# Two transformer blocks with 32 experts on one core: the last pairs of experts in another order, and part of the last normalisation on GpSimd and ScalarE

## The chip, the core and the metric

The kernel runs on one NeuronCore of a Trainium2 chip. Its engines are TensorE (PE, matrix products), VectorE (DVE), ScalarE (ACT), GpSimd (Pool) and SyncE (SP, which here issues DMAs). The metric is the device time of one execution in microseconds (us), smaller is better.

## What is computed

The reference runs two blocks over 512 tokens of 1024 numbers in float32. The first is a mixer block of depth 2, the second has two kinds of attention and ends with a mixture of 32 experts, a sum and a last normalisation. Only this end matters here:

```python
def _rmsnorm(x, g):
    x32 = x.astype(jnp.float32)
    y = x32 * lax.rsqrt(jnp.mean(x32 * x32, axis=-1, keepdims=True) + EPS)
    return (y * g.astype(jnp.float32)).astype(x.dtype)
...
    for e in range(N_EXPERTS):
        he = jax.nn.silu(xt @ w_gate[e]) * (xt @ w_up[e])
        y = y + combine[:, e:e + 1] * (he @ w_down[e])
    return y
...
        x = x + y.reshape(B, T, D)
    return _rmsnorm(x, final_norm)
```

Each token goes to two of the 32 experts.

## The kernel before

The experts are worked through one after the other, in a list sorted so that each has room for 128, 96, 64 or 32 of its tokens. Weights come by DMA from SP's queue some experts ahead, the tokens of an expert by an indirect DMA from Pool's queue. The names used below:

- `gu(e)`: the gate and up products of expert `e`. For a small expert the result `pgu` is split over groups of rows and copied to `eg` by ACT (line 1843).
- `fold(e)`: PE transposes `eg` into `pfold` (line 1850), DVE sums it to `ef` (line 1852), ACT takes a tanh, and DVE makes the hidden row `eh` in two operations (lines 1861, 1862).
- `turn(e)`: PE transposes the gathered tokens of the next expert.
- `pair(e)`: the down products of two experts of the same size, `pyf` (line 1890). ACT scales them into `ys` (line 1897) and DVE makes a second tile with what the first lost in rounding, called the correction below (line 1899). Experts with 32 rows fill a quarter of such a tile each, so the pairs 28 and 29 and 30 and 31 share one.
- `add(n)`: takes up to `n` items off a list. An item is one full tile of results and one of the four tiles of 128 tokens: four PE products with a selection matrix, `psel` (line 1917), and two DVE additions to the tokens `xk` (line 1919).
- `back_add(t)`: two DVE additions of rows that the larger experts scattered to memory (line 2053).
- `finish`: for each of four tiles of tokens the last adds, then ACT's sum of squares (line 1931). Behind the fourth tile `FT` puts the inverse root, ten small DVE operations in `rsq` (lines 233 to 242), and then for each tile one DVE operation that multiplies by the root and the final weights `fin` into `fo` (line 1939), and the DMA of `fo` to the output from SP's queue.

From expert 3 on the order of PE is that of the program, written by hand; a scheduler arranges the other engines' operations and PE's after the last pair. Each engine executes its own list strictly in order. After the last tile comes a loop over experts that overflowed (`overflow`), which all engines enter and leave together.

Of the kernel before, what the change touches and what calls it, by code (L numbers as in the profile page):

```python
# [14 lines left out]
AF = mybir.ActivationFunctionType  # L15
OP = mybir.AluOpType
# [8 lines left out]
NE = 32  # L25
# [4 lines left out]
UNIT = 1040  # L30
PTC = 2
PS2 = (3, 2, 2)
FT = ((0, 4, 3),)
HB = 2

# [77 lines left out]
class K:  # L113
# [40 lines left out]
    def pb(self, name="pb"):  # L154
        return self.ps.tile([128, 512], F32, name=name, tag="A", bufs=PS2[0]) if self.single else self.pa(name)[:, :512]

# [6 lines left out]
    def pt(self, name="ptr"):  # L163
        return self.ps.tile([128, 512], F32, name=name, tag="T", bufs=PS2[1] if self.single else 2)

    def pc(self, name="pc"):
        return self.ps.tile([128, 512], F32, name=name, tag="C", bufs=PS2[2] if self.single else 1)

# [1752 lines left out]
    def finish(self, add):  # L1921

        nc = self.nc
        raw = self.eraw
        fs = raw("fs")[:, :8].rearrange("p (a t) -> p a t", a=2)
        os = []
        for t in range(4):
            add(t)
            x = self.xk[:, t, :]
            o = raw("fo")  # L1930
            nc.scalar.activation(o, x, AF.Square, accum_out=fs[:, 0, t:t + 1])
            os.append(o)
            for a, b, at in FT:
                if at != t:
                    continue
                self.rsq(fs[:, 1, a:b], fs[:, 0, a:b], 1.0 / D, EPS)
                for u in range(a, b):
                    o, rs = os[u], fs[:, 1, u:u + 1]
                    nc.vector.scalar_tensor_tensor(o, self.xk[:, u, :], rs, self.fin, op0=OP.mult, op1=OP.mult)  # L1939
                    nc.sync.dma_start(self.out[0, u * 128:(u + 1) * 128, :], o)  # L1940

    def moe(self):
        nc, I, sp, tc = self.nc, self.I, self.sp, self.tc
# [25 lines left out]
        def load(e):  # L1969
            if e + LA < NE:  # L1970
                U[e + LA] = self.ex_load(e + LA, w_of(0, e + LA), w_of(1, e + LA))
            if e + WH < NE:
                Dn[e + WH] = self.ex_wd(w_of(2, e + WH))
# [5 lines left out]
        def turn(e):  # L1979
            if e < NE:  # L1980
                X[e] = self.ex_turn(xgs[e % 2], mp, cap[e], e < 2)
# [13 lines left out]
        def gu(e):  # L1995
            if cap[e] > 64:
                Hs[e] = self.ex_gu(U[e], X[e], mp)
            else:
                G[e] = self.ex_half(U[e], X[e], mp, cap[e])

        def fold(e):
            if cap[e] <= 64:
                Hs[e] = self.ex_fold(G[e], mp, cap[e])
# [22 lines left out]
        def pair(e):  # L2026

            n = cap[e]
            q, b, sel, parts = S.pop(n, (0 if n > 32 else nm, 0, None, None))
            if b == 0:  # L2030
                sel = mp.tile([128, 512], F32R, name="sel", tag="sel", bufs=SB)
                self.ex_select(sel, by[:, 0, q:q + 1])
                parts = [mp.tile([128, 1024], F32, name="ys", tag="ys", bufs=YB).bitcast(F32R) for _ in range(2)]
            r = slice(b, b + 2 * n)
            py = self.ex_few([Dn[e - 1], Dn[e]], [Hs[e - 1], Hs[e]], n)
            self.ex_parts(py, by[r, 1, q:q + 1], [p[r] for p in parts])
            if b + 2 * n < 128:
                S[n] = q, b + 2 * n, sel, parts
            else:
                S[n] = q + 1, 0, None, None  # L2040
                return sel, parts, 128
# [3 lines left out]
        def back(t):  # L2045

            for k in range(2):
                y = B[t, k] = self.eraw("yb")
                nc.sync.dma_start(y, self.yd[k * 512 + t * 128:k * 512 + t * 128 + 128, :])
# [12 lines left out]
        def add(n):  # L2062

            for x in waiting[:n]:
                self.ex_add(*x)
            del waiting[:n]

        def step(e):
            nonlocal full
            load(e)  # L2070
            if e + 1 < NE:
                gu(e + 1)
            full = None
            if cap[e] > 64:
                scatter(e)
            elif cap[:e + 1].count(cap[e]) % 2 == 0:
                full = pair(e)
            turn(e + 2)
            gather(e + 4)
            add(2 if cap[min(e + 1, NE - 1)] > 32 else 1)  # L2080
            if e + 1 < NE:
                fold(e + 1)
            if e == 1:
                rows_by()
            if e == 15:
                self.route_extra(mp)
            if RB <= e <= RB + 1:
                back(e - RB)
            if RB < e <= RB + 2:
                back_add(e - RB - 1)  # L2090
            if full and e + 1 < NE:
                waiting.extend(full + (t,) for t in range(4))
# [3 lines left out]
        with tc.manual_schedule(engines={mybir.EngineType.PE}):  # L2096
            for e in range(3, END):
                step(e)
            load(END)
            for t in (2, 3):  # L2100
                back(t)
            for e in range(END + 1, NE):
                gu(e)
                turn(e + 1)
                add(1)
                fold(e)
            add(4)
            pair(NE - 3)
            full = pair(NE - 1)

        def last(t):
# [78 lines left out]
```

## Time and profile before

| | before |
|---|---|
| median of 3 runs | 1414.97 us (1413.94 to 1420.77) |
| the profiled execution | 1415.46 us |
| its span in the trace | 1413.6 us |
| PE, DVE busy | 1291.6 us (91%), 947.3 us (67%) |
| ACT, Pool busy | 611.2 us (43%), 311.0 us (22%) |

The span runs from the first instruction of the program to the last; all times below count from its start. A timeline row gives start, length, engine, line, operation, output and inputs, shapes and number of operations, and in brackets how long the engine stood idle before it and what ended that.

### The profile page before, as it was taken

What the parts mean: (1) busy time and instruction counts of PE and PEld (TensorE: products, weight loads), DVE (VectorE), ACT (ScalarE), POOL (GpSimd) and SP (SyncE); (2) the same over time, 40 slices, a digit from 0 to 9 for tenths busy, and PEclk for the clock granted to TensorE, in tenths of its full rate; (3) what the DMA queues carried; (4) which work ended last, traced back from release to release, by engine and by line L of the source; (5) the groups of instructions that cost most, each with busy time, mean ns of one, the idle gap of its engine ahead of it and who ended that gap; (6) DMA issues with size and microseconds to landing.
All of it is one profiled execution on the core that took longest, in us unless ns stands there. A gap on an engine that the chain in (4) does not pass through costs nothing. (4 is left out here: it accounts for less than half of the span.)

```text
span 1413.6 us, 22394 instructions
## 1 busy us (share of the span) xinstructions
PE 1291.6 (91%) x7974; PEld 1026.3 (73%) x7974; DVE 947.3 (67%) x2113; ACT 611.2 (43%) x1197; POOL 311.0 (22%) x412
## 2 busy tenths in 40 slices
PE   4999999999989999799999999999999799989792
PEld 2888778877768788677877778787788766765461
DVE  5789998566743689998775554676667723554565
ACT  4554165445641564256573334776654211112122
POOL 5333032322220233133322110211110121111100
PEclk9999999999999999999999999999999799989996
DMA  9643355435132344426144355324424799998992
GB/s 343 159 134 109 97 150 156 132 109 172 60 134 64 98 128 146 136 55 160 31 134 148 112 192 152 87 73 139 137 73 168 258 383 383 371 373 325 395 407 83
DMA packets 166772, 246.18 MB, mean 174 GB/s; under 512 B 46788, under 2 KB 102810, under 8 KB 166660
## 3 DMA queue, kind: packets, MB, share of 16 engines
q1 hardware_dynamic: 161116, 234.95, 49.9%
q0 software_dynamic: 4864, 7.66, 2.0%
q10 hardware_dynamic: 680, 2.13, 0.4%
q8 instruction: 64, 1.05, 0.3%
q14 instruction: 48, 0.39, 0.1%
HBM read 220.69 MB, written 32.28 MB: 179 GB/s over the span
## 5 line engine op out<-in xcount | busy, mean ns | idle before, releaser
L185 DVE TENSOR_TENSOR wlo<-wraw,whi 128x1024 fp32r<-128x1024 f32 (+3 forms) x98 | 118.2, 1212 | 59.5 <-ACT whi L184 59.0
L184 ACT ACTIVATE whi<-wraw 128x1024 fp32r<-128x1024 f32 (+3 forms) x98 | 100.7, 1036 | 102.3 <-PE pout L223 42.7
L221 PE MATMUL pcm<-hTh,whi 128*128 128x256 f32 (+1 forms) x288 | 102.1, 355 | 8.4 <-DVE oa L531 4.3
L571 DVE SCALAR_TENSOR_TENSOR za<-zp,vec,za 128x783 f32<-128x783 f32 (+1 forms) x120 | 108.9, 915 | 0.5
L923 POOL TENSOR_SCALAR P<-P,ll 128x768 f32<-128x768 f32 (+1 forms) x80 | 73.5, 924 | 159.7 <-DVE ll L922 142.6
L223 PE MATMUL pcm<-hTh,wlo 128*128 128x256 f32 (+1 forms) x288 | 98.4, 342 | 0.1
L222 PE MATMUL pcm<-hTl,whi 128*128 128x256 f32 (+1 forms) x288 | 97.9, 340 | 0.0
L185 DVE TENSOR_TENSOR PTl<-pPT,PTh 128x512 fp32r<-128x512 f32 x104 | 70.3, 684 | 25.2 <-ACT PTh L184 24.6
L921 ACT ACTIVATE P<-pS,nm 128x768 f32<-128x768 f32 (+1 forms) x80 | 65.0, 816 | 36.2 <-DVE nm L919 30.7
L184 ACT ACTIVATE PTh<-pPT 128x512 fp32r<-128x512 f32 x104 | 60.7, 596 | 45.3 <-PE pPT L936 41.1
L1812 POOL DMA_INDIRECT xg<-h2d,tok x32 | 31.5, 983 | 219.9 <-PE pturn L1796 165.1
L1418 POOL TENSOR_SCALAR P<-P,l 128x384 f32<-128x384 f32 (+1 forms) x64 | 33.2, 534 | 185.8 <-DVE l L1417 168.7
L919 DVE TENSOR_REDUCE nm<-pS 128x1 f32<-128x768 f32 (+1 forms) x80 | 66.0, 843 | 9.3 <-PE pS L223 8.5
L221 PEld LDWEIGHTS pcm<-hTh,whi 128*128 128x128 f32 x288 | 54.7, 190 | 16.3 <-DVE oa L531 4.9
L221 PE MATMUL pcm<-hT0h,whi 128*128 128x512 f32 x144 | 59.3, 412 | 7.9 <-DVE oa L531 5.8
L936 PE MATMUL pPT<-ident,P 128*128 128x128 f32 x416 | 62.5, 279 | 0.9 <-DVE PTl L185 0.4
L223 PEld LDWEIGHTS pcm<-hTh,wlo 128*128 128x128 f32 x288 | 54.6, 190 | 6.4 <-DVE wlo L185 0.6
L968 POOL TENSOR_TENSOR oa<-oa,ot 64x256 f32<-64x256 f32 x40 | 37.4, 935 | 97.4 <-DVE ot L967 94.1
L222 PEld LDWEIGHTS pcm<-hTl,whi 128*128 128x128 f32 x288 | 54.8, 190 | 5.1 <-issue 0.5
L222 PE MATMUL pcm<-hT0l,whi 128*128 128x512 f32 x144 | 58.3, 405 | 0.0
L223 PE MATMUL pcm<-hT0h,wlo 128*128 128x512 f32 x144 | 58.2, 404 | 0.0
L1829 PE MATMUL pgu<-exT,eraw 128*128 128x128 f32 x448 | 55.8, 289 | 0.0
(552 smaller groups left out, 3645.2 us busy)
## 6 DMA issues: line engine op xcount, KB each, us to landing
wraw<-in_w_in_dram SPq DMA_DIRECT2D x56, 512.0 KB, 4.6
eraw<-in_w_expert_gate_dram SPq DMA_DIRECT2D x52, 512.0 KB, 10.1
eraw<-in_w_expert_up_dram SPq DMA_DIRECT2D x52, 512.0 KB, 10.4
wraw<-in_w_mod_dram SPq DMA_DIRECT2D x48, 512.0 KB, 5.6
wl<-in_w_expert_down_dram SPq DMA_DIRECT2D x32, 512.0 KB, 6.4
wh<-in_w_expert_down_dram SPq DMA_DIRECT2D x32, 512.0 KB, 11.0
wraw<-in_w_out_dram SPq DMA_DIRECT2D x24, 512.0 KB, 3.6
wraw<-in_w_expert_gate_dram SPq DMA_DIRECT2D x12, 512.0 KB, 13.1
```

Source lines behind the costliest of these rows:

```text
L184: nc.scalar.activation(hi, src, AF.Copy)
L185: return (eng or nc.vector).tensor_tensor(lo, src, hi.bitcast(F32), op=OP.subtract)
L221: mm(out, lhs[0], rhs[0], start=start, stop=False)
L222: mm(out, lhs[0], rhs[1], start=False, stop=False)
L223: mm(out, lhs[1], rhs[0], start=False, stop=stop)
L571: nc.vector.scalar_tensor_tensor(a[:, :nz], z[:, k:k + nz], cfw[:, i, k:k + 1], a[:, :nz], op0=OP.mult, op1=OP.add)
L919: nc.vector.tensor_reduce(nm, S, axis=AX.X, op=OP.max, negate=True)
L921: nc.scalar.activation(P, S, AF.Exp, bias=nm, accum_out=l)
L923: nc.gpsimd.tensor_scalar(P, P, l, 0.5, op0=OP.mult, op1=OP.mult)
L936: nc.tensor.transpose(p[:, jj, i * 128:(i + 1) * 128], Ps[i][:, (j + jj) * 128:(j + jj + 1) * 128], self.ident)
L968: nc.gpsimd.tensor_tensor(o, o, t, op=OP.mult)
L1829: self.last = self.nc.tensor.matmul(p[:, s, c, :], gu[2 * s + k // 4][:, k % 4, c * 128:(c + 1) * 128], x[:, k, :], start=(k == 0), stop=( ...
```

## The change

In the loop over the last three experts, each step that still has another expert behind it now takes two items off the list instead of one. The last step takes none; the pair of experts 28 and 29 is done there, before the last folding, and what is left of the list behind it. In `finish`, for the first two of the four tiles, Pool multiplies the tokens by the final weights as soon as the square is taken (in the same tile `fo`, which the square leaves), and when the root is there ACT scales that product. The other two tiles are as before.

```diff
+FV = (0, 0, 1, 1)
...
             nc.scalar.activation(o, x, AF.Square, accum_out=fs[:, 0, t:t + 1])
+            if not FV[t]:
+                nc.gpsimd.tensor_tensor(o, x, self.fin, op=OP.mult)
             os.append(o)
...
                     o, rs = os[u], fs[:, 1, u:u + 1]
-                    nc.vector.scalar_tensor_tensor(o, self.xk[:, u, :], rs, self.fin, op0=OP.mult, op1=OP.mult)
+                    if FV[u]:
+                        nc.vector.scalar_tensor_tensor(o, self.xk[:, u, :], rs, self.fin, op0=OP.mult, op1=OP.mult)
+                    else:
+                        nc.scalar.activation(o, o, AF.Copy, scale=rs)
                     nc.sync.dma_start(self.out[0, u * 128:(u + 1) * 128, :], o)
...
             for e in range(END + 1, NE):
                 gu(e)
                 turn(e + 1)
-                add(1)
+                if e < NE - 1:
+                    add(2)
+                else:
+                    pair(NE - 3)
                 fold(e)
-            add(4)
-            pair(NE - 3)
+            add(9)
             full = pair(NE - 1)
```

PE's list from the adds of expert 30's step to the end of the last pair, before:

```order
L1917 MATMUL psel<-ys,sel 128x512 x4
L1850 MATMUL pfold<-ident,eg 128x128 x4
L1840 MATMUL pgu<-eraw,exT 32x256 x16
L1917 MATMUL psel<-ys,sel 128x512 x4
L1850 MATMUL pfold<-ident,eg 128x128 x4
L1917 MATMUL psel<-ys,sel 128x512 x8
L1890 MATMUL pyf<-wh,eh 32x512 x4
L1890 MATMUL pyf<-wl,eh 32x512 x4
L1890 MATMUL pyf<-wh,eh 32x512 x4
L1890 MATMUL pyf<-wl,eh 32x512 x4
```

and now:

```order
L1918 MATMUL psel<-ys,sel 128x512 x8
L1851 MATMUL pfold<-ident,eg 128x128 x4
L1841 MATMUL pgu<-eraw,exT 32x256 x16
L1891 MATMUL pyf<-wh,eh 32x512 x4
L1891 MATMUL pyf<-wl,eh 32x512 x4
L1851 MATMUL pfold<-ident,eg 128x128 x4
L1918 MATMUL psel<-ys,sel 128x512 x4
L1891 MATMUL pyf<-wh,eh 32x512 x4
L1891 MATMUL pyf<-wl,eh 32x512 x4
```

Lines of the changed kernel are higher by one here. The first pair's down products (`pyf`) stand behind the last gate and up product and ahead of the last folding (`pfold`); four of the adds' products (`psel`) stand between the folding and the last pair, where before there were twelve around the folding. The step before, for expert 29, has eight such products instead of four in the same way.

DVE's list from the last folding's sum to the adds of the last pairs, before:

```order
L1852 TENSOR_REDUCE ef<-pfold 128x4x32
L1919 TENSOR_TENSOR xk<-psel,xk 128x512
L1861 SCALAR_TENSOR_TENSOR eh<-eh,ef 128x64
L1919 TENSOR_TENSOR xk<-psel,xk 128x512
L1862 TENSOR_TENSOR eh<-ef,eh 128x64
L1919 TENSOR_TENSOR xk<-psel,xk 128x512 x2
L1899 SCALAR_TENSOR_TENSOR ys<-pyf,by,ys 64x512 x4
L1919 TENSOR_TENSOR xk<-psel,xk 128x512 x4
L2053 TENSOR_TENSOR xk<-xk,yb 128x1024 x4
```

and now:

```order
L1853 TENSOR_REDUCE ef<-pfold 128x4x32
L1920 TENSOR_TENSOR xk<-psel,xk 128x512
L1900 SCALAR_TENSOR_TENSOR ys<-pyf,by,ys 64x512 x2
L1862 SCALAR_TENSOR_TENSOR eh<-eh,ef 128x64
L1920 TENSOR_TENSOR xk<-psel,xk 128x512
L1863 TENSOR_TENSOR eh<-ef,eh 128x64
L1900 SCALAR_TENSOR_TENSOR ys<-pyf,by,ys 64x512 x2
L1920 TENSOR_TENSOR xk<-psel,xk 128x512 x4
L2059 TENSOR_TENSOR xk<-xk,yb 128x1024 x4
```

The first pair's two corrections (`ys`) stand ahead of both operations of the last hidden row (`eh`), where before all four corrections came behind it. On Pool two products `fo<-xk,fin` of 128x1024 stand behind the last gather and nothing but the loop's end follows them; on ACT two scalings of `fo` follow the four squares.

## Rows read from the trace of the kernel before

**Rows 1.** Timeline of PE, the last pairs of experts.

```profile
1373.26 1.93 PE L1840 MATMUL pgu<-eraw,exT 128*32 128x256 f32 x32
1375.12 1.19 PE L1917 MATMUL psel<-ys,sel 128*128 128x512 f32 x4
1376.16 0.60 PE L1850 MATMUL pfold<-ident,eg 128*128 128x128 f32 x4
1376.51 2.09 PE L1917 MATMUL psel<-ys,sel 128*128 128x512 f32 x8
1378.53 1.07 PE L1890 MATMUL pyf<-wh,eh 128*32 128x512 f32 x8
...
1380.27 1.04 PE L1890 MATMUL pyf<-wh,eh 128*32 128x512 f32 x8
```

**Rows 2.** Timeline of DVE, from the last folding to the scattered rows.

```profile
1377.09 0.68 DVE L1852 TENSOR_REDUCE ef<-pfold 128x128 f32<-128x512 f32 x1
1377.69 0.68 DVE L1919 TENSOR_TENSOR xk<-psel,xk 128x512 f32<-128x512 f32 x1
1378.29 0.22 DVE L1861 SCALAR_TENSOR_TENSOR eh<-eh,ef 128x64 f32<-128x64 f32 x1
...
1379.02 0.22 DVE L1862 TENSOR_TENSOR eh<-ef,eh 128x64 f32<-128x64 f32 x1
...
1381.96 1.51 DVE L1899 SCALAR_TENSOR_TENSOR ys<-pyf,by,ys 64x512 fp32r<-64x512 f32 x2 [1.53 <-ACT ys L1897]
1383.66 1.54 DVE L1899 SCALAR_TENSOR_TENSOR ys<-pyf,by,ys 64x512 fp32r<-64x512 f32 x2 [0.19 <-ACT ys L1897]
1385.23 2.48 DVE L1919 TENSOR_TENSOR xk<-psel,xk 128x512 f32<-128x512 f32 x4
1387.63 4.62 DVE L2053 TENSOR_TENSOR xk<-xk,yb 128x1024 f32<-128x1024 f32 x4
```

**Rows 3.** Timeline of DVE: a root at the start of the kernel, and the end.

```profile
15.44 0.91 DVE L235 TENSOR_SCALAR hrs<-rt 128x2 int32<-128x2 int32 x1
...
1395.86 0.17 DVE L233 TENSOR_SCALAR rv<-fs 128x4 f32<-128x4 f32 x1 [1.22 <-ACTq L2129]
...
1397.86 4.87 DVE L1939 SCALAR_TENSOR_TENSOR fo<-xk,fs,fin 128x1024 f32<-128x1024 f32 x4
```

**Rows 4.** Stretches: PE, PEld, DVE, ACT, POOL busy (operations), PE's clock, DMA share, GB/s.

```profile
1400.00:1405.00 5.00, 0.00 (x0) 0.00 (x0) 2.73 (x3) 0.00 (x0) 0.00 (x0) 0.50 1.02 406
...
1390.70:1413.60 22.90, 0.00 (x0) 0.00 (x0) 10.47 (x20) 2.30 (x4) 0.00 (x0) 0.50 0.23 92
```

**Rows 5.** Timeline of ACT, the last pairs and the first square.

```profile
1380.55 1.38 ACT L1897 ACTIVATE ys<-pyf,by 64x512 fp32r<-64x512 f32 x2 [2.48 <-PE pyf L1890]
1382.24 1.39 ACT L1897 ACTIVATE ys<-pyf,by 64x512 fp32r<-64x512 f32 x2 [0.31 <-PE pyf L1890]
1386.55 1.06 ACT L1931 ACTIVATE fo<-xk 128x1024 f32<-128x1024 f32 x1 [2.92 <-DVE xk L1919]
```

**Rows 6.** Groups of Pool's instructions by form: count, busy us, mean ns, idle before.

```profile
L624 POOL TENSOR_TENSOR g<-g,scv 128x768 f32<-128x768 f32 x2 | 3.7, 1831 | 14.8 <-DVE g L531 14.8
...
L624 POOL TENSOR_TENSOR g<-g,scv 128x512 f32<-128x512 f32 x2 | 2.5, 1273 | 1.7 <-DVE g L531 1.7
```

**Rows 7.** Timeline of DVE and Pool from 57.0 to 61.2.

```profile
57.09 1.22 DVE L425 TENSOR_TENSOR hTl<-x,hTh 128x1024 fp32r<-128x1024 f32 x1
57.47 3.83 POOL L867 TENSOR_TENSOR ra<-lat,tabk 128x32 f32<-128x32 f32 x1 [9.99 <-ACT lat L456]
...
60.23 0.96 DVE L185 TENSOR_TENSOR wlo<-wraw,whi 128x768 fp32r<-128x768 f32 x1
```

**Rows 8.** Timeline of DVE and Pool from 535.7 to 538.

```profile
535.93 1.55 POOL L853 TENSOR_TENSOR kt<-krot,hr 128x256 f32<-128x256 f32 x1 [3.61 <-DVE hr L242]
536.92 1.11 DVE L852 TENSOR_TENSOR kt<-kt,hr 128x512 f32<-128x512 f32 x1
```

**Rows 9.** All instructions on the tile `kt`: DVE's, ns least/median/most, first and last start.

```profile
L852 DVE TENSOR_TENSOR kt<-kt,hr x12: 679/693/1109, 79.9 to 587.9; 128x512 f32<-128x512 f32 x12
```

## The prediction

> **What bounds the kernel now.** The page's totals decide nothing here, since the change touches only the end, so I went to the timeline of the last 40 us, engine by engine. TensorE (PE) goes without a pause from experts to token adds and to the down products of the last two pairs [rows 1]. Then VectorE (DVE) runs the end: from the corrections of those pairs at 1381.96 on its operations stand almost back to back, with one gap of 1.53 us before them and one of 0.19 us between the pairs [rows 2]. The inverse root starts at 1395.86 and the four normalised tiles at 1397.86 [rows 3]. After that the writes to memory are the limit: from 1400 to 1405 they move 406 GB/s at a full DMA share [rows 4]. So there are two questions: when does DVE get to 1397.86, and when can the first write be issued?
>
> **Part 1: the order of the last pairs.** No operation is added or removed; eight PE products for adds move earlier and the pair of experts 28 and 29 moves ahead of the last folding. I walk PE and then DVE with the gaps of the rows. Eight add products instead of four hold PE 2.02 us (1376.51 to 1378.53) instead of 1.04 (1375.12 to 1376.16), so each of two steps is 0.98 later and the last gate-and-up product starts at 1373.26 + 1.96 = 1375.22 [rows 1]. It takes 1.86 (to 1375.12 before), so the moved pair's down products start at 1377.08, 1.45 earlier than 1378.53. They take 1.74 (1378.53 to 1380.27), the folding starts at 1378.82 instead of 1376.16, and it is done 0.60 later, at 1379.42 [rows 1].
>
> Now DVE, which executes in the order shown above: reduction, add, both row corrections of the moved pair, first half of the last hidden row, add, second half. The reduction goes at 1379.42, the add at 1380.02 and free again at 1380.62, each 0.60 after the one before [rows 2]. The corrections need ACT's copies, which come 2.02 after the products start (1378.53 to 1380.55) and take 1.38 [rows 1, 5]: ready at 1380.48, so they cost no wait. They occupy 1.51, to 1382.13 [rows 2]. Hidden row and add take 0.73 (1378.29 to 1379.02) and the second half of the hidden row 0.22 [rows 2]: the last hidden row is ready at 1383.08 instead of 1379.24. Before, the last pair's products started at 1380.27 because PE was busy until then [rows 1]; now they start at about 1383.1, because PE waits for DVE. From there the chain is the old one (1.97 to ACT's copies, 1.42 to the corrections, 1.57 to the adds [rows 1, 2, 5]), so everything from 1385.23 on comes **2.84 us later** (1383.11 less 1380.27). What was meant to be pulled ahead is pulled ahead, but its 1.51 us on DVE now stands in front of the hidden row on which the last pair hangs. Nothing hides it: DVE stands idle afterwards, waiting for the last pair.
>
> PE stands idle for some 2.7 us in this wait. Its clock can fall in it: from 1390.7 on, when PE has no more products, the granted clock is 0.50, which is 1.2 GHz [rows 4]. If the last pair's products ran at that level instead of 2.4 GHz they would take twice their 1.74 us. So this term lies between 0 and 1.74. I take 0, because the products come at the end of the idle stretch and not long after it, and keep 1.74 for the range.
>
> **Part 2: the products on Pool.** Two tiles' multiplications by the final weights go to Pool, which is idle after its last gather, and they need no scale, so they can run while DVE adds. The trace has no Pool product of 128x1024; 128x512 takes 1.27 and 128x768 takes 1.83 [rows 6], 0.56 more for each 256 columns, so I take 2.39 each. The first may start when the first tile's square is done, at 1387.61 (1386.55 + 1.06 [rows 5]) and a little for its read-out, just as DVE begins the four adds of the scattered rows (1387.63, 4.62 us for four [rows 2]). Both engines then read two operands from SBUF. The trace shows what that does, in two ways. At 57.47 a Pool product of 32 columns took 3.83 us, until the last of four such DVE operations (57.09 to 60.23) was over; those were not held up, the first took 1.22 and the last 0.96 [rows 7]. At 535.93 Pool got in between two DVE operations: it took 1.55, and DVE's second took 1.11 [rows 8], where the median of 12 is 0.69 [rows 9]. So they exclude each other, and who gets the turn decides the price.
>
> I take the first way: Pool is shut out until DVE's four adds end at 1392.25 (1387.63 + 4.62). The next four DVE adds read one operand from PSUM, and Pool runs beside them. Its two products then end at 1392.25 + 4.78 = 1397.03. The inverse root would start at 1395.86, and its small steps wait too: at 15.44 one of them took 0.91 [rows 3] beside a Pool product, where the first step at the end takes 0.17 [rows 3]. So the root starts at 1397.03: **1.17 us later**. The bounds are 0 (Pool disturbs nothing) and 4.78 (both products go ahead of a DVE add and DVE waits their whole length).
>
> The Trainium skill, on its page "SBUF — State Buffer", section "Who interferes with whom", says that a DVE instruction with two SBUF inputs contends with a GpSimd instruction that reads SBUF, and that whichever issues first holds the shared ports for its whole instruction. By that rule Pool, which asks before each following add, would get its turn twice and the term would be 4.78. The rows at 57.47 speak against first come, first served; those at 535.93 agree with it.
>
> **Part 3: the end.** ACT scales the two products where DVE took 1.22 us each (4.87 for four [rows 3]). ACT's square over the same 128x1024 takes 1.06 [rows 5], so the first tile is ready **0.16 earlier**, and the second 1.06 after it. Two of four DVE operations, 2.44 us, fall away, but this is worth nothing: a tile of 0.52 MB takes 1.29 us to write at 406 GB/s [rows 4], so the second to fourth tiles wait for the writes, not for an engine. SP's queue holds the same four writes in the same order; no DMA is added. If Pool were late, ACT's scaling and all four writes behind it on SP would wait, but Pool ends before the root does. What follows the last write until 1413.6 is unchanged.
>
> **The sum.** 2.84 + 1.17 - 0.16 = +3.85 us. The profiled execution took 1415.46, 0.49 above the median, and would take 1419.3; against the median of 1414.97 I forecast 1418.8.
>
> **The rivals.**
> Pool gets one turn. The first product goes between two adds, as at 535.93, and DVE is 2.39 late; the second ends at 1397.03, before the root then starts at 1398.25, and costs nothing. 2.84 + 2.39 - 0.16 = +5.07: 1420.0. For it: Pool asks almost as the first add begins (1387.61 and 1387.63 [rows 2, 5]), and where it was shut out at 57.47 it had asked 0.38 us after the operation then running. Against it: at 57.47 three changes from one DVE operation to the next went by without a turn [rows 7].
>
> Pool gets two turns, and the kernel is **slower**. Place: the four adds of scattered rows; price 2 x 2.39; it decides from the point where both products stand ahead of an add. 2.84 + 4.78 - 0.16 = +7.46: 1422.4, which is 0.53% more. For and against as above, only twice.
>
> Pool disturbs nothing, because its read and DVE's happen not to meet: 2.84 - 0.16 = +2.68: 1417.7. Against it: the long operations of [rows 7, 8].
>
> The gain that the change is made for. If the hidden row is not held up (because the products or copies come earlier than I reckon, so that DVE's corrections fall into an idle time), the gaps of 1.53 and 0.19 vanish and Pool is free: -1.72 - 0.16 = -1.88: 1413.1. Against it: DVE's order is fixed, and the corrections stand ahead of the hidden row in it.
>
> That the split does not do what it says is in the forecast already: two of four DVE operations go, and the writes keep the end where it was.
>
> **How the numbers follow.** Forecast 0.40, one turn 0.25, two turns 0.13, no disturbance 0.12, gain 0.10. The clock adds up to 1.74 to each but the last. A measurement of this kernel can tell about 0.5% from no change, 7.1 us here. Slower by more needs two turns (0.10 of its 0.13) or one turn with most of the clock's loss (5.07 + 1.74, and a little noise: 0.03): 0.13. Faster by more has no case; 0.02 for what I do not see. The rest, 0.85, is no change. The range leaves out most of the gain below, and above it the two turns with a slower clock: 1414.2 to 1422.8.
>
> **What would show it.** Right: the moved pair's products near 1377.1, the last pair's near 1383.1 with PE idle for over 2 us before it, and DVE idle for about 3.5 us before the last corrections; the first Pool product far longer than 2.4 us, the adds of scattered rows still 1.14 apart, the root held back by about a microsecond; writes at 406 GB/s from end to end. Wrong in part 1 if the last pair's products start before 1381. Wrong in part 2 if an add of scattered rows takes over 2 us, or if Pool's products last 2.4 us from the start and no DVE operation is longer.

## The result, and the profile after

| | before | changed |
|---|---|---|
| median | 1416.68 us (20 runs, 1413.07 to 1422.79) | 1425.74 us (20 runs, 1419.85 to 1429.86) |
| the profiled execution | 1415.46 us | 1429.09 us |
| its span | 1413.6 us | 1427.3 us |

The ratio is 1.0055, 95% interval [1.0042, 1.0068]: the change makes the kernel some 7.8 us slower (5.9 to 9.6 by the interval). The two medians lie 9.06 us apart. I had forecast +3.85 us, with a range up to 1422.8, so the forecast and the range were both wrong. The rival "Pool gets two turns" (+7.46) is what happened.

The two profiled executions cannot be compared by their spans. The program is the same up to the step of expert 29, and yet that step's gate and up products start 6.26 us later in the profile after. The first row is before, the others are after.

```profile
1365.18 1.93 PE L1840 MATMUL pgu<-wraw,exT 128*32 128x256 f32 x32
```

```profile
1371.44 1.93 PE L1841 MATMUL pgu<-wraw,exT 128*32 128x256 f32 x32
...
1383.13 1.04 PE L1891 MATMUL pyf<-wh,eh 128*32 128x512 f32 x8
...
1384.96 0.66 PE L1851 MATMUL pfold<-ident,eg 128*128 128x128 f32 x4
...
1386.47 1.04 PE L1891 MATMUL pyf<-wh,eh 128*32 128x512 f32 x2
1389.40 0.63 PE L1891 MATMUL pyf<-wh,eh 128*32 128x512 f32 x3 [1.88 <-DVE eh L1863]
```

From here on I measure everything from the start of these products and call what follows the **tail**: 48.45 us before (1413.6 less 1365.18) and 55.84 after. The difference of 7.39 us is the effect of the change in these two executions, and it lies inside the interval of the ratio. The timeline of DVE after shows both places where it comes from:

```profile
1385.65 0.69 DVE L1853 TENSOR_REDUCE ef<-pfold 128x128 f32<-128x512 f32 x1 [2.10 <-PE pfold L1851]
1386.26 0.68 DVE L1920 TENSOR_TENSOR xk<-psel,xk 128x512 f32<-128x512 f32 x1
1386.86 1.50 DVE L1900 SCALAR_TENSOR_TENSOR ys<-pyf,by,ys 64x512 fp32r<-64x512 f32 x2
1388.28 0.21 DVE L1862 SCALAR_TENSOR_TENSOR eh<-eh,ef 128x64 f32<-128x64 f32 x1
1388.52 0.69 DVE L1920 TENSOR_TENSOR xk<-psel,xk 128x512 f32<-128x512 f32 x1
1389.13 0.21 DVE L1863 TENSOR_TENSOR eh<-ef,eh 128x64 f32<-128x64 f32 x1
1392.80 1.54 DVE L1900 SCALAR_TENSOR_TENSOR ys<-pyf,by,ys 64x512 fp32r<-64x512 f32 x2 [3.45 <-ACT ys L1898]
1394.37 2.48 DVE L1920 TENSOR_TENSOR xk<-psel,xk 128x512 f32<-128x512 f32 x4
1396.77 8.91 DVE L2059 TENSOR_TENSOR xk<-xk,yb 128x1024 f32<-128x1024 f32 x4
1405.60 2.47 DVE L1920 TENSOR_TENSOR xk<-psel,xk 128x512 f32<-128x512 f32 x4
1409.28 0.17 DVE L234 TENSOR_SCALAR rv<-fs 128x4 f32<-128x4 f32 x1 [1.22 <-ACT fo L1932]
```

First place: the moved pair's corrections (1386.86) stand ahead of the last hidden row (1389.13). Two of the last pair's sixteen products go at 1386.47 already; the others wait for that row, PE idles for 1.88 us, and they start 17.96 us into the tail (1389.40 less 1371.44). Before, the last pair's products started 15.09 into it (1380.27 [rows 1] less 1365.18). That is 2.87 us later, and DVE then idles for 3.45 us. Second place: the four adds of scattered rows take 8.91 us where before they took 4.62 [rows 2]. The timeline in narrower windows shows the four one by one, and then Pool's two products:

```profile
1396.77 1.22 DVE L2059 TENSOR_TENSOR xk<-xk,yb 128x1024 f32<-128x1024 f32 x1
1397.90 3.36 DVE L2059 TENSOR_TENSOR xk<-xk,yb 128x1024 f32<-128x1024 f32 x1
1401.18 3.35 DVE L2059 TENSOR_TENSOR xk<-xk,yb 128x1024 f32<-128x1024 f32 x1
1404.46 1.21 DVE L2059 TENSOR_TENSOR xk<-xk,yb 128x1024 f32<-128x1024 f32 x1
```

```profile
1396.92 3.26 POOL L1934 TENSOR_TENSOR fo<-xk,fin 128x1024 f32<-128x1024 f32 x1 [25.80 <-ACT fo L1932]
1400.14 3.31 POOL L1934 TENSOR_TENSOR fo<-xk,fin 128x1024 f32<-128x1024 f32 x1
```

Read them together. Pool's first product asks at 1396.92, while the first add runs. When that add ends, at 1397.99 (1396.77 + 1.22), Pool is served (I call this being let in, or getting a turn): its product ends at 1400.18, 2.2 us later, and only then does the second add proceed, which takes 3.36 instead of 1.22. Pool's second product asks at 1400.14, waits for the second add and is served ahead of the third. A row's length holds the waiting too, on both engines.

The clock (as a share of 2.4 GHz) and the writes, in windows of the profile after, with the columns of [rows 4]:

```profile
1383.13:1389.40 6.27, 4.39 (x30) 1.59 (x22) 4.03 (x9) 2.11 (x4) 0.00 (x0) 1.00 0.57 226
1389.40:1396.77 7.37, 6.03 (x28) 2.79 (x28) 3.91 (x7) 2.44 (x4) 0.00 (x0) 1.00 0.02 8
...
1413.50:1418.50 5.00, 0.00 (x0) 0.00 (x0) 0.26 (x1) 0.03 (x1) 0.00 (x0) 0.50 1.02 406
```

The granted clock stays at its upper level of 2.4 GHz through PE's wait and behind it, and the writes again run at 406 GB/s, as in [rows 4].

### The profile page after: what moved, and what is told of

Read it like the earlier page. It is cut to its first block, busy times and chain, and to the rows that moved or that the text cites. A ratio compares the mean times of both kernels' runs of the same rounds, so it can differ in the third digit from the quotient of the medians.

```text
span 1427.3 us, 22401 instructions
## 1 busy us (share of the span) xinstructions
PE 1298.4 (91%) x7974; PEld 1032.0 (72%) x7974; DVE 949.4 (67%) x2111; ACT 613.2 (43%) x1199; POOL 318.4 (22%) x414
```

## The experiments

One table for all, from the traces. "Pair" is the start of the last pair's products (in the new order without the two that are done early), "adds" the length of the four adds of scattered rows, "root" the start of the inverse root; pair, root and the end of the tail count from the start of expert 29's gate and up products. A run without a ratio was executed once, with its profile.

| run | pair | adds | root | tail | ratio to before [95%] |
|---|---|---|---|---|---|
| before | 15.09 | 4.62 | 30.69 | 48.45 | |
| changed | 17.96 | 8.91 | 37.84 | 55.84 | 1.0055 [1.0042, 1.0068] |
| order alone | 17.96 | 4.62 | 33.55 | 51.31 | 1.0026 [1.0009, 1.0042] |
| split alone | 15.09 | 8.91 | 34.97 | 52.98 | 1.0024 [1.0003, 1.0044] |
| one product | 15.09 | 6.76 | 32.83 | 50.53 | |
| asked later | 15.09 | 8.91 | 34.97 | 52.98 | 1.0029 [1.0006, 1.0051] |
| held | 15.09 | 4.62 | 30.68 | 50.15 | |
| one operand | 15.09 | 6.30 | 32.35 | 50.37 | |
| free adds | 15.09 | | 33.78 | 51.80 | |
| parts after | 16.40 | 4.62 | 32.02 | 49.78 | |
| pieces | 15.09 | 6.20 | 32.26 | 50.28 | |
| two early adds | 16.03 | | 31.44 | 49.22 | 1.0008 [0.9993, 1.0024] |
| one early add | 15.10 | | 29.78 | 47.55 | 0.9996 [0.9979, 1.0012] |
| small piece first | 15.09 | 8.90 | 34.96 | 53.06 | |

### The two halves apart

Order alone is the changed kernel with the old end:

```diff
-FV = (0, 0, 1, 1)
+FV = (1, 1, 1, 1)
```

> The new order of the last pairs, with all four tiles' products of the last norm by DVE as before. Measured from the start of the gate and up product of expert 29, the tail lasts 48.4 us in the kernel before and 55.8 us in the change. Theory (the two halves of the change add up, 2.9 us from the order and 4.3 us from Pool): last pair's down products 2.8 us later than before, the four adds of scattered rows 4.6 us together as before, tail 51.2 us (+2.8), median about +3 us. Rival (the order costs nothing, it is all Pool): tail 48.4 us. Rival (the order brings a lower clock behind it): tail above 52 us with a granted clock below 1.00 ahead of the last adds.

Split alone is the changed kernel with the loop of before:

```diff
-                if e < NE - 1:
-                    add(2)
-                else:
-                    pair(NE - 3)
+                add(1)
                 fold(e)
-            add(9)
+            add(4)
+            pair(NE - 3)
```

> The order of before, with only the products of tiles 0 and 1 on Pool and their scaling on ACT. Theory (Pool takes two turns between the four adds): adds 8.9 us together instead of 4.6, the root 4.3 us later, tail 52.7 us (+4.3), median about +4.5 us. The step that I forecast (Pool is shut out until the adds end): adds 4.6 us, root +1.2 us, tail 49.6 us. Rival (Pool takes its turns only because the new order brings the adds to a moment that suits it): adds 4.6 to 6.8 us here.

The rows of the order alone, PE's and DVE's:

```profile
1384.06 0.63 PE L1891 MATMUL pyf<-wh,eh 128*32 128x512 f32 x3 [1.88 <-DVE eh L1863]
```

```profile
1391.42 4.62 DVE L2059 TENSOR_TENSOR xk<-xk,yb 128x1024 f32<-128x1024 f32 x4
```

Measured: +2.86 us from the order and +4.53 us from the split (51.31 and 52.98 less 48.45). Their sum is 7.39, what the whole change costs: the two halves do not help or hinder each other. Of the split's 4.53, 4.28 are in the root's start already (34.97 less 30.69), all of it in the four adds; the last 0.25 come behind the root. I did not follow them up; with one product on Pool (below) they are not there (17.70 us from the root to the end, 17.76 before). The rows of DVE and Pool in the split alone are those of the changed kernel again, though its adds begin at another moment of the program:

```profile
1385.84 8.91 DVE L2059 TENSOR_TENSOR xk<-xk,yb 128x1024 f32<-128x1024 f32 x4
```

```profile
1386.00 6.53 POOL L1934 TENSOR_TENSOR fo<-xk,fin 128x1024 f32<-128x1024 f32 x2 [22.94 <-ACT fo L1932]
```

### What the order costs: the corrections

The pair's down products stay in the new place, but the scaling and the corrections are asked for behind the last folding (order alone with this edit):

```diff
-            self.ex_parts(py, by[r, 1, q:q + 1], [p[r] for p in parts])
+            todo = (py, by[r, 1, q:q + 1], [p[r] for p in parts])
+            if held is None:
+                self.ex_parts(*todo)
+            else:
+                held.append(todo)
...
-                    pair(NE - 3)
+                    pair(NE - 3, held)
...
             add(9)
+            self.ex_parts(*held[0])
```

> The new order of the tensor engine, all four tiles by DVE, but the moved pair's scaling and its two corrections are asked for behind the last folding. Theory (the 2.86 us of the order alone come mostly of the two corrections of 1.51 us that DVE does ahead of the last hidden row): the last pair's down products 0.7 to 1.3 us later than in the kernel before, tail 49.1 to 49.8 us. Rival (the place of the moved products on the tensor engine itself costs it): last pair 2.8 us later, tail 51.3 us.

```profile
1380.15 0.21 DVE L1862 SCALAR_TENSOR_TENSOR eh<-eh,ef 128x64 f32<-128x64 f32 x1
...
1380.89 0.21 DVE L1863 TENSOR_TENSOR eh<-ef,eh 128x64 f32<-128x64 f32 x1
1381.02 1.50 DVE L1900 SCALAR_TENSOR_TENSOR ys<-pyf,by,ys 64x512 fp32r<-64x512 f32 x2
1384.55 1.54 DVE L1900 SCALAR_TENSOR_TENSOR ys<-pyf,by,ys 64x512 fp32r<-64x512 f32 x2 [2.03 <-ACT ys L1898]
```

Now the hidden row (1380.15, 1380.89) stands ahead of the corrections (1381.02). The pair comes 1.31 us late instead of 2.87, and the tail is 49.78: 1.53 of the 2.86 us, a little over half, went with them, and the corrections take 1.50. ACT's scaling moved along, but it is not what the row waited for: in the profile after ACT had finished its tanh 1.6 us before the first half of the hidden row (1388.28):

```profile
1386.40 0.24 ACT L1861 ACTIVATE eh<-ef 128x64 f32<-128x64 f32 x1
```

The other 1.33 us are what is left with the products in front of the folding on PE; no run takes that part away by itself. So the theory holds at the upper end of what I expected.

### What the split costs: one turn per product

Only tile 0's product on Pool, in the split alone:

```diff
-FV = (0, 0, 1, 1)
+FV = (0, 1, 1, 1)
```

> As the split alone, but only tile 0's product on Pool, tile 1's by DVE. Theory (each Pool product holds DVE up for one turn of 2.15 us): adds 6.8 us, tail about 50.6 us (+2.1). Rival (the first clash alone costs, whatever number follows): adds 8.9 us, tail 52.7 us. Rival (only the second product is let in between): adds 4.6 us.

```profile
1394.95 6.76 DVE L2059 TENSOR_TENSOR xk<-xk,yb 128x1024 f32<-128x1024 f32 x4
```

One product lengthens the adds by 2.14 us (6.76 for 4.62), two by 4.29, twice that: about 2.15 us for each, as the theory had it. The tail is 50.53.

Then the case that I had forecast, made by hand. Pool first copies a column behind the last add, so that it cannot ask earlier:

```diff
-                nc.gpsimd.tensor_tensor(o, x, self.fin, op=OP.mult)
+                pass
...
+            for u in range(2):
+                nc.gpsimd.tensor_copy(os[u][:, 0:1], self.xk[:, 3, 0:1])
+                nc.gpsimd.tensor_tensor(os[u], self.xk[:, u, :], self.fin, op=OP.mult)
```

> As the split alone, but Pool first copies one column of tile 3 behind the last of the four adds, so that both products begin only there: the case that I had forecast, made by hand. Theory (Pool's products cost DVE nothing once its own two-operand adds out of SBUF are over, and a product that holds nobody up takes about 2.2 us, as the turns of 2.15 us in the split alone say): adds 4.6 us together, the products done some 5 us after the last add began, the root at 30.7 us from the gate and up product of expert 29 as before, tail 48.2 to 49.6 us. Rival (the last four adds out of PSUM alternate with Pool too): root 2 to 4.3 us later, tail 50.5 to 52.7 us.

```profile
1390.56 4.62 DVE L2066 TENSOR_TENSOR xk<-xk,yb 128x1024 f32<-128x1024 f32 x4
1395.10 2.47 DVE L1920 TENSOR_TENSOR xk<-psel,xk 128x512 f32<-128x512 f32 x4
1398.79 1.63 DVE L234 TENSOR_SCALAR rv<-fs 128x4 f32<-128x4 f32 x1 [1.22 <-ACT fo L1939]
```

```profile
1395.74 4.66 POOL L1932 TENSOR_TENSOR fo<-xk,fin 128x1024 f32<-128x1024 f32 x2
```

The adds are undisturbed at 4.62, the adds out of PSUM run beside Pool at 2.47 as before, and Pool's two products take 4.66. But they end at 1400.40, and the root's first step, which takes 0.17 elsewhere, takes 1.63: it waits for Pool. The tail is 50.15, +1.70, above the 48.2 to 49.6 that I expected: a product took 2.35 and not 2.2, and with the two copies ahead the first began only 0.56 us behind the last add (1395.74 less 1395.18).

Last, each product of the split alone cut in four:

```diff
-                nc.gpsimd.tensor_tensor(o, x, self.fin, op=OP.mult)
+                for j in range(0, D, 256):
+                    nc.gpsimd.tensor_tensor(o[:, j:j + 256], x[:, j:j + 256], self.fin[:, j:j + 256], op=OP.mult)
```

> As the split alone, but each Pool product is cut into four of 256 columns. Theory (Pool is let in once at each end of an add and DVE waits for the whole operation that it lets in, about 0.55 us for 256 columns by the 2.15 us of 1024): three turns of 0.55 us, adds 6.2 to 6.4 us, the rest of the pieces beside the adds out of PSUM without holding them up, tail about 50.1 us (+1.7). Rival (DVE pays for the sum of Pool's work however it is cut): adds 8.9 us, tail 52.9 us.

```profile
1391.26 1.74 DVE L2060 TENSOR_TENSOR xk<-xk,yb 128x1024 f32<-128x1024 f32 x1
```

```profile
1396.88 2.78 POOL L1935 TENSOR_TENSOR fo<-xk,fin 128x256 f32<-128x256 f32 x4
```

Three adds are 0.53 us longer each (1.74 for 1.22), the adds take 6.20, the tail 50.28, which is still 1.83 more than before. The fourth piece goes in behind the last add, the four that are left run beside the adds out of PSUM, and the root waits for none (they end at 1399.66, it starts at 1399.94). DVE pays for what is let in between its operations, not for Pool's work as a whole.

### Why is Pool let in here, and was not at 57.47?

My forecast leaned on the Pool product at 57.47 [rows 7], which was passed over three times. Three theories of what made that place different were tried, each in the split alone.

Time of asking: Pool writes half a tile before its first product, so that it asks later.

```diff
+                if t == 0:
+                    nc.gpsimd.memset(o[:, 0:512], 0.0)
                 nc.gpsimd.tensor_tensor(o, x, self.fin, op=OP.mult)
```

> As the split alone, but Pool first writes half of tile 0's output (128x512), so that it asks for its first product some 0.5 us later, well inside the first add instead of 0.16 us after its start. Theory (what decides a turn is who asks first: DVE asks for its next add about 0.16 us into the running one, and Pool that comes later is passed over until the adds end): adds 4.6 to 4.8 us, both products behind them, tail 48.4 to 49.8 us. Rival (Pool is let in at the next end of an add whenever it asked): adds 8.9 us as in the split alone, tail 52.7 us.

```profile
1389.86 0.53 POOL L1935 MEMSET fo<- 128x512 f32 x1 [22.91 <-DVE xk L1920]
1390.48 5.95 POOL L1936 TENSOR_TENSOR fo<-xk,fin 128x1024 f32<-128x1024 f32 x2
```

```profile
1389.73 8.91 DVE L2061 TENSOR_TENSOR xk<-xk,yb 128x1024 f32<-128x1024 f32 x4
```

Pool asks 0.75 us into the first add (1390.48 less 1389.73) and is let in all the same: 8.91 us. The theory falls. The write to SBUF alone took 0.53 us beside the running add and disturbed nothing.

DVE's own results: the four adds replaced by products that wait for no earlier result of DVE.

```diff
-                BE[k](nc).tensor_tensor(xk[:, t, :], xk[:, t, :], B[t, k], op=OP.add)
+                if t > 1:
+                    BE[k](nc).tensor_tensor(B[t, k], B[t, k], self.fin, op=OP.mult)
...
```

> As the split alone, but DVE's four adds of scattered rows become products of those rows with the norm's weight, which wait for their transfers and for nothing that DVE itself wrote (the scattered rows are left out of tiles 2 and 3). They now stand as two pairs with two of the adds out of PSUM behind each. Theory (DVE gives its turn away because each of the adds waits for an earlier result of DVE's own; without that wait it keeps the turn, as in the row of before where Pool was passed over three times): the second of the first pair takes 1.2 us, and Pool comes in behind the pair. Rival (Pool comes in at the end of the running operation here too): the second of the first pair takes 3.36 us.

```profile
1389.23 3.36 DVE L2060 TENSOR_TENSOR yb<-yb,fin 128x1024 f32<-128x1024 f32 x1
...
1393.71 2.17 DVE L2060 TENSOR_TENSOR yb<-yb,fin 128x1024 f32<-128x1024 f32 x1
```

The second of the first pair takes 3.36 us: Pool is let in here too, and this theory falls as well. Its second product runs on beside the two adds out of PSUM, and the third product of DVE (1393.71) waits only for what was left of it.

Size: tile 0's product in a piece of 32 columns and one of 992.

```diff
-                nc.gpsimd.tensor_tensor(o, x, self.fin, op=OP.mult)
+                for j in ((0, 32), (32, D)) if t == 0 else ((0, D),):
+                    nc.gpsimd.tensor_tensor(o[:, j[0]:j[1]], x[:, j[0]:j[1]], self.fin[:, j[0]:j[1]], op=OP.mult)
```

> As the split alone, but tile 0's product on Pool is cut into a first piece of 32 columns and one of 992 columns, to see why a Pool product of 32 columns was passed over three times at 57.47 in the kernel before. Theory (a piece as small as that is passed over): the piece ends behind the adds, adds 4.6 us, tail 50 us or more because the rest comes late. Rival (size does not matter, each piece is let in at the next end of an add): one add longer by about 0.1 to 0.3 us, two by about 2.1 us each, adds 9.0 to 9.3 us, tail about 53 us.

```profile
1388.93 1.17 POOL L1935 TENSOR_TENSOR fo<-xk,fin 128x32 f32<-128x32 f32 x1 [22.93 <-ACT fo L1932]
```

The small piece goes in at the end of the first add (it is done 1.17 us after it asked), the second add is 0.05 longer (1.27 for 1.22), the third and the fourth take 3.29 and 3.36. The third theory falls too.

What can be said: the outcome goes with the place in the program, and is not chance. In the fourteen traces of this study the product of 57.47 took 3.79 to 3.83 us every time, and Pool's products at the end were let in at every end of an add at which one waited. Nor does 57.47 stand alone. The sharpest comparison is [rows 8] with an earlier place in the same trace, where the same operation of Pool asks 0.16 us into an equal operation of DVE (0.15 at 535.93) and the same one of DVE follows:

```profile
117.75 3.00 POOL L853 TENSOR_TENSOR kt<-krot,hr 128x256 f32<-128x256 f32 x1 [16.20 <-DVE hr L242]
```

```profile
118.72 0.69 DVE L852 TENSOR_TENSOR kt<-kt,hr 128x512 f32<-128x512 f32 x1
```

There Pool is passed over twice and DVE's operation takes its 0.69; at 535.93 Pool is let in and it takes 1.11. All fourteen traces show both outcomes at these two places. So neither the kind and size of the operations nor the time of asking tells them apart. What in the place decides stays open.

### One operand instead of two

```diff
-                nc.gpsimd.tensor_tensor(o, x, self.fin, op=OP.mult)
+                nc.gpsimd.tensor_scalar(o, x, 1.0, None, op0=OP.mult)
```

> As the split alone, but Pool multiplies tiles 0 and 1 by the number 1 and not by the norm's weight, so it reads one operand in place of two (the weight is left out of these two tiles). Theory (a Pool operation that reads SBUF excludes DVE's adds, whatever the count of its operands): two of the adds longer by 1.0 to 1.2 us each, adds 6.6 to 7.0 us, tail about 50.6 us. Rival (only two operands clash): adds 4.6 us, both Pool operations beside them, tail 48.3 us.

```profile
1390.57 2.05 DVE L2059 TENSOR_TENSOR xk<-xk,yb 128x1024 f32<-128x1024 f32 x1
```

Two of the adds are longer by 0.84 us each (2.05 for 1.21), the adds take 6.30. So a Pool operation with one operand from SBUF holds DVE's adds up too, for less time. I had expected 1.0 to 1.2.

### Work for DVE's idle time

The 1.53 us of idle time that [rows 2] shows ahead of the corrections could take work that DVE must do anyway. First try: in the kernel before, the moved pair between the last folding and `add(4)`, and two of the four scattered adds ahead of the last pair's corrections. `half_add` is one of the two additions of `back_add`, and what stands under `issue_after` is put behind it.

```diff
-            add(4)
             pair(NE - 3)
-            full = pair(NE - 1)
+            add(4)
+            half_add(2, 0)
+            with tc.issue_after(half_add(2, 1).ins):
+                full = pair(NE - 1)
```

> No Pool product and no split. The pair of experts 28 and 29 goes behind the last folding but ahead of the four adds, so that the last hidden row is not behind its corrections, and the first two adds of scattered rows are done ahead of the last pair's corrections. Theory (the 1.72 us in which DVE is idle in the kernel before are filled with work that it has to do anyway): last pair's corrections up to 1 us later, then only two scattered adds behind them, root 0.7 to 1.7 us earlier than 30.7 us, tail 46.7 to 47.8 us, ratio 0.9988 to 0.9995, which the runs can hardly tell from 1. Rival (the scattered rows have not landed by then and DVE waits for their transfers): a gap of DVE that ends on a transfer, tail 48.4 us or more.

Missed: the root comes 0.75 us later. It is not the rival either, since no wait of DVE ends on a transfer. The moved products of PE push the eight products of four adds behind them, and DVE waits for those:

```profile
1380.15 1.29 DVE L1919 TENSOR_TENSOR xk<-psel,xk 128x512 f32<-128x512 f32 x2 [0.74 <-PE psel L1917]
```

PE in turn comes to the last pair 0.94 us later (16.03 for 15.09). The gap has moved, and not gone. Besides, the four adds in a row take 4.62 us in [rows 2], where the two pairs here take 2.48 and 2.47. Each pair is the two adds of one tile, the second of which needs the result of the first.

Second try: PE's order untouched, one add in the gap.

```diff
             add(4)
-            pair(NE - 3)
-            full = pair(NE - 1)
+            with tc.issue_after(half_add(2, 0).ins):
+                pair(NE - 3)
+                full = pair(NE - 1)
```

> The order of the tensor engine of the kernel before, all four tiles by DVE, and one of the four adds of scattered rows done ahead of both last pairs' corrections, in the 1.53 us in which DVE is idle there. The choosing of the last pairs' rows (0.48 us for 128x512, elsewhere in the trace of before) stands behind it in DVE's order, so 1.70 us of work go into 1.53 us. Theory (that idle time is free for work that must be done anyway, and the 0.19 us between the pairs takes up what is late): three adds remain behind the corrections, root 0.7 to 1.1 us earlier than 30.7 us, tail 47.3 to 47.8 us; too little for the times of the runs to tell from no change. Rival (as in the kernel with two early adds, breaking up rows of operations costs DVE what the gap gives): root within 0.3 us of before or later.

```profile
1382.27 1.23 DVE L2052 TENSOR_TENSOR xk<-xk,yb 128x1024 f32<-128x1024 f32 x1 [0.19 <-DMA yb<-yd]
1383.41 0.48 DVE L1909 TENSOR_SCALAR sel<-io,by 128x512 fp32r<-128x512 f32 x1
1383.80 3.07 DVE L1899 SCALAR_TENSOR_TENSOR ys<-pyf,by,ys 64x512 fp32r<-64x512 f32 x4
```

All four corrections follow without a gap, the root is 0.91 us earlier and the tail 47.55, 0.90 less than before. It is the shortest tail of all kernels here, though the add waited 0.19 us for its transfer. The tail is that of one execution; in the times no gain can be told: 0.9996 [0.9979, 1.0012].

## Why the prediction was wrong

**Part 1, the order: right, in place and size.** Forecast +2.84 us for the last pair's products, because DVE does the moved pair's corrections ahead of the last hidden row; measured 2.87 at that place and 2.86 in the tail. PE's wait came, but shorter than the 2.7 us (at least 2) that I gave for it: 1.88, because two of the last pair's products did not need the row and went ahead. The clock's loss that I had kept for the range (up to 1.74) did not occur: the granted clock is 1.00 in both windows. That the corrections' 1.51 us stand in front is shown by the kernel that takes them away (1.53). That the rest comes from the folding's later place on PE is only what remained there.

**Part 2, Pool: wrong.** The step that failed is "I take the first way: Pool is shut out until DVE's four adds end". Pool was let in at the end of the first add and of the second. The term was +4.28 at the root, not +1.17. Both rows that I had weighed were real, and one of them, [rows 8], showed the other outcome; the trace before shows it in other places as well, here at 287.20, with Pool's row first and DVE's under it:

```profile
287.20 1.23 POOL L968 TENSOR_TENSOR oa<-oa,ot 64x256 f32<-64x256 f32 x1 [1.14 <-DVE ot L967]
```

```profile
287.08 0.75 DVE L608 SCALAR_TENSOR_TENSOR scv<-u,vec,scv 128x512 f32<-128x512 f32 x1
287.75 1.09 DVE L185 TENSOR_TENSOR vhl<-vraw,vhl 128x384 fp32r<-128x384 f32 x1
```

There DVE's second operation takes 1.09, and 0.54 where nobody stands in its way. I gave the one row at 57.47 the weight of a rule and never said what in it made Pool wait, which I still cannot say. The trace before has both outcomes, each in several places (117.75 and 287.20 are two), and did not choose between them. The chances of one and two turns together, 0.38, were nearly that of the forecast; but one turn for two products was a rival without a row of its own. The price that I had for two turns was good: 4.78 forecast, 4.28 measured, since a product holds DVE for 2.15 us and not for 2.39. And being shut out would not have been cheap either: the held kernel, with two copies of a column ahead, pays 1.70 for it.

The Trainium skill, on "SBUF — State Buffer", section "Who interferes with whom", says that an instruction of Pool that reads SBUF and one of DVE with two inputs there exclude each other, and that one that only writes does not. These runs agree: 2.15 us per product, nothing for the 0.53 us write, nothing for the adds out of PSUM. Its sentence that issue order decides who blocks gives the two turns seen here, and not the three that Pool was refused at 57.47.

**Part 3, the end: right that it gains next to nothing, wrong in sign.** Forecast -0.16. The scaling on ACT took 2.19 for two tiles, 1.1 each, and the first write went out 0.1 us earlier after the root; the writes ran at 406 GB/s as before. The split leaves the end 0.25 us later and not earlier, for a cause that stays open.

**The rivals.** Two turns was +7.46 by my working; the tail says +7.39. That is in part luck: 4.28 for 4.78 and 0.25 for -0.16 nearly cancel, so that it fits better than its terms do.

**The range.** Its top was 1422.8, just above the two turns at 1422.4. The changed kernel's median, 1425.74, lies above it even though the mechanism stands in the rivals. Of the 3.3 us over 1422.4, 1.71 are the kernel before, which came out higher in 20 runs (1416.68) than in the three that I had (1414.97). The rest is that the medians differ by 9.06 us where the tails differ by 7.39, in runs of either kernel that spread over some 10 us. A range from a median of three should have been wider by that.

## What to carry to other kernels

Before an idle Pool is given work that reads SBUF, look at what DVE does in that moment: if it runs long operations with two inputs from SBUF, price both outcomes. Pool may be let in after each of them, and DVE then pays the length of what is let in; or Pool may be passed over, and what needs its result waits. A row from another place in the program does not tell which. If the work must go to Pool, pieces cost DVE less (0.53 us per turn instead of 2.15, though here still 1.83 us in all), and beside adds out of PSUM it cost DVE nothing; keep it clear of the small steps on the critical path. And when work is pulled ahead on one engine, look at what follows it on the others: here 1.5 us of corrections came along and stood in front of the one row that the next products needed.

## What was not expected of the hardware

- A step of DVE on 128x4 numbers with one input took 1.63 us instead of 0.17 while Pool's product was running (1398.79 in the held kernel), and ended 0.02 us after it. The forecast had reckoned with such a wait from the row at 15.44 [rows 3]; my expectation for the held kernel had not.
- Pool's operation with one input cost each of two adds 0.84 us, and let an undisturbed add through between them; its two operations took turns with the second and the fourth add, where the products with two inputs took them with the second and the third.
- In fourteen profiles the same places always gave the same outcome: Pool was passed over at 57.47 and 117.75, and let in at 535.93 and at the end. Neither the time of asking nor the size nor DVE's own results explain it.
